# A hybrid encoder layer on one core: the last output columns in three pieces, and the scalings behind them put in another order

## The chip, the cores and the metric

The kernel runs on one core of one Trainium2 chip. The time is the device time of one execution in microseconds. Five engines work side by side, each on its own list of instructions: TensorE (PE in the profile, its weight loads PEld), VectorE (DVE), ScalarE (ACT), GpSimd (POOL) and SyncE (SP), which here only issues transfers. Engines wait for one another on semaphores.

## What is computed

One layer over 528 tokens (16 learned ones and 512 of the input) of width 2048. Cut to what matters:

```python
hn = rmsnorm(h_res, norm_in_g)              # (528, 2048)
P  = hn @ w_in                              # 2048 x 8320
y_a = rwkv7 time mixing of P[:, :4224], 16 heads of 64, gated with silu
y_b = Bg * causal_conv3(Cg * hc) * silu(g_c) of P[:, 4224:]
mix = concatenate([y_a, y_b])               # (528, 2048)
h_res = h_res + mix @ w_out                 # 2048 x 2048
out = rmsnorm(h_res, norm_f_g)[16:]         # (512, 2048), f32
```

The last line is where the change lies: each output row is scaled by one over the root of the mean of its squares (plus 1e-6), and each column by its entry of `norm_f_g`. A row's scale is known only when all its 2048 columns are.

## The kernel before

All matmuls with large operands keep f32 accuracy by splitting: an operand is `hi` (its value rounded to the type float32r) plus `lo` (the rest), and a product is three matmuls, hi by hi, hi by lo and lo by hi. The profile calls such operands f32 as well; where a cast writes one it says fp32r. One instruction on TensorE takes a weight tile of 128x128 and streams up to 512 columns over it, into a bank of PSUM.

The input projection and the recurrence take up to about 850 us, and TensorE goes through them almost without a gap. Then comes the output projection, `mix @ w_out`, in two halves of 1024 columns. Each half is a Strassen-like scheme of seven products (`M1`, `P5`, `M7`, `M3`, `Q6`, `P4`, `M2`) over blocks of 256 rows and 512 columns; a product is summed over 1024 rows of `w_out` in eight steps `jj`, three matmuls a step. `close` adds a finished product to the tiles that hold the residual: `xa[t]` for the first 1024 columns of row block `t` (four blocks of 128 tokens), `xb[m][:, t]` for the two further groups of 512. `here(t, n)` is row block `t`, column group `n` (0 to 3). `gfb` holds `norm_f_g`, the columns' factors, on all partitions.

The change is in the end of the program, from line 1400 on, behind all products but the last one, `M2` of the second half. Its weights (`right[(1, "M2", ..)]`, tiles named `home`) were split ahead of time. It adds to column group 2 of row blocks 0 and 1 only, so row blocks 2 and 3 are complete before it. The steps there:

- L1220 (called at L1403): `M2` for row block 0, 24 matmuls of 512 columns into `end`.
- `row_part` (L1364, L1365) sums the squares known so far into `fv[:, t, 0:1]`; `row_scale` (L1372, then the power at L101 on GpSimd) adds the last part and takes the power of minus one half. Its result is the row's scale `r`.
- `finish(t, ns)`: for column groups 2 and 3 one instruction on VectorE that multiplies with `r` and the factors (L1382); for group 0, which stands for the first 1024 columns, one on ScalarE (L1385), their factors having been applied earlier on GpSimd. Each is followed by its transfer to DRAM on SP's queue (L1386).
- L1411: the addition of `end` to row block 0; `squares(0, 2)` (L1207) squares it on ScalarE and sums along the row.
- L1415: the factors (`gain`, L1278) for row block 1, column group 3.
- L1416 to L1431: `M2` for row block 1 in two pieces of 256 columns, 24 matmuls each (L1422). Behind each piece its addition (L1426), its squares (L1207) and its factors (L1278). Between the two, behind the first piece, row block 0 is scaled and sent (`finish(0, (2, 0, 3))`), and L1431 adds the first piece's squares to the sum.
- `row_scale(1, 4)` on VectorE and GpSimd, and `finish_last(1)`: the four column groups of row block 1 are scaled, two on VectorE (L1391, L1396), one on ScalarE (L1393), one on GpSimd (L1395), with a transfer each, two from SP's queue (L1392, L1397) and two from ScalarE's (L1394, L1398).

The order of instructions on VectorE, ScalarE, GpSimd and TensorE is here that of the program text (`manual_schedule`); on SP it follows too. Each engine works its list strictly in order, so an instruction that waits holds up all behind it on its engine.

Of the kernel before, what the change touches and what calls it, by code (L numbers as in the profile page):

```python
# [9 lines left out]
F32 = mybir.dt.float32  # L10
# [3 lines left out]
ALU = mybir.AluOpType  # L14
# [4 lines left out]
P = 128  # L19
DM = 2048  # L20
# [56 lines left out]
def hymba_kernel(ctx: ExitStack, tc: tile.TileContext, xt, xtok, front, w_in, w_out, pv, lup, cst, msk, gf, out):  # L77
    nc = tc.nc
# [21 lines left out]
    def rsqrt(y, v):  # L100
        nc.gpsimd.tensor_tensor(out=y, in0=v, in1=mhalf[:, 0 : v.shape[1]], op=ALU.pow)  # L101
# [10 lines left out]
    for what, i in plan:  # L112
        m = tile_of[what] + i
# [109 lines left out]
    o = 0  # L223
# [61 lines left out]
    with tc.issue_after(head):  # L285
        nc.vector.tensor_scalar(
            out=omm, in0=pvt[:, V_MU : V_MU + 33], scalar1=-1.0, scalar2=1.0, op0=ALU.mult, op1=ALU.add
        )
        for d, off in (
# [4 lines left out]
                out=d, in0=pvt[:, off : off + 8], scalar1=0.5, scalar2=None, op0=ALU.mult  # L294
            )
        nc.vector.tensor_scalar(
            out=hv[:, 4], in0=pvt[:, V_KA : V_KA + 8], scalar1=-0.5, scalar2=1.0, op0=ALU.mult, op1=ALU.add
# [825 lines left out]

    pw = ctx.enter_context(tc.tile_pool(name="pw", bufs=1, reuse_waits="tile"))
    po = ctx.enter_context(tc.tile_pool(name="po", bufs=8, space=PSUM, reuse_waits="tile"))
    ssq = pw.tile([P, 4, 5], F32, name="ssq")
    fv = pw.tile([P, 4, 3], F32, name="fv")
    sform = {
        (f, q): [pw.tile([P, 4, HT], F32R, tag=f"{f}{q}{a}", name=f"{f}{q}{a}") for a in range(2)]
# [14 lines left out]
    for half in range(2):  # L1144
        units += [(half, "M1", g) for g in range(4)]
        units += [(half, prod, g) for g in range(4) for prod in ("P5", "M7", "M3", "Q6")]
        ends = ("P4", 0), ("P4", 1), ("M2", 0), ("P4", 2), ("M2", 1), ("P4", 3), ("M2", 2), ("M2", 3)
# [4 lines left out]
    def left(prod, jj, part, s):  # L1152
        w = LEFT[prod]
        tk = slice(s * P, (s + 1) * P)
        if isinstance(w, str):
            return sform[w, jj // 4][part][:, jj % 4, tk]
        if w == 0:
            return parts[jj][part][:, tk]
        return parts[NPAIR + jj][part][:, w][:, tk]
# [36 lines left out]
    def here(t, n):  # L1196
        return xa[t][:, n * 512 : (n + 1) * 512] if n < 2 else xb[n - 2][:, t]

    def onto(t, n, ps, op):
        h = here(t, n)  # L1200
        nc.vector.tensor_tensor(out=h, in0=h, in1=ps, op=op)

    def squares(t, n, part=None):
        o = slice(0, 512) if part is None else slice(256 * part, 256 * part + 256)
        sq = pw.tile([P, 512], F32, tag="sqj", name=f"sqj{n}_{t}_{part}")
        j = (0, 1, 3, 2)[n] + (part or 0)
        nc.scalar.activation(sq[:, o], here(t, n)[:, o], AF.Square, scale=DM**-0.5, accum_out=ssq[:, t, j : j + 1])  # L1207

    def gain(t, n, eng, o=slice(0, 512)):
        h = here(t, n)[:, o]  # L1210
        eng.tensor_tensor(out=h, in0=h, in1=gfb[:, n * 512 : (n + 1) * 512][:, o], op=ALU.mult)

    def product(unit, bank, s_):
        half, prod, g = unit
        for s in s_:
            for q in range(2):
                jj = 2 * g + q
                hi, lo = right[unit, q]
                for n, (m, w) in enumerate(((0, hi), (0, lo), (1, hi))):
                    nc.tensor.matmul(  # L1220
                        bank[s], left(prod, jj, m, s), w, start=(jj == 0 and n == 0), stop=(jj == 7 and n == 2)
                    )
# [4 lines left out]
    def close(half, prod, z):  # L1227
        n = 2 * half
        if prod == "M1":
            shared[:] = [pw.tile([P, 512], F32, tag=f"sh{s}", name=f"sh{half}{s}") for s in range(2)]  # L1230
        for s in range(2):
            d, p, t = shared[s], z[s], 2 + s
            if prod == "M1":
                nc.scalar.copy(d, p)
                onto(s, n, p, ALU.add)
            elif prod == "P5":
                onto(t, n + 1, p, ALU.subtract)
                onto(s, n + 1, p, ALU.subtract)
            elif prod == "M7":
                onto(t, n + 1, p, ALU.subtract)  # L1240
                onto(t, n, p, ALU.add)
            elif prod == "M3":
                onto(s, n + 1, p, ALU.subtract)
            elif prod == "Q6":
                nc.vector.tensor_tensor(out=d, in0=d, in1=p, op=ALU.add)
                for r, c, op in ((t, n, ALU.add), (t, n + 1, ALU.subtract), (s, n + 1, ALU.subtract)):
                    onto(r, c, d, op)
                squares(t, n + 1)
                squares(s, n + 1)
            elif prod == "P4":  # L1250
                onto(t, n, p, ALU.add)
                squares(t, n)
            else:
                onto(s, n, p, ALU.add)
                squares(s, n)
# [42 lines left out]
    for half in range(2):  # L1298
        o = 28 * half
# [62 lines left out]
    def row_part(t, n):  # L1362
        w = fv[:, t, 0:1]
        nc.vector.tensor_reduce(out=w, in_=ssq[:, t, 0:n], op=ALU.add, axis=AX.X)  # L1364
        nc.vector.tensor_scalar(out=w, in0=w, scalar1=RMS_EPS, scalar2=None, op0=ALU.add)  # L1365
# [3 lines left out]
    def row_scale(t, n, eng=nc.gpsimd):  # L1369
        f = fv[:, t]  # L1370
        w, v, r = f[:, 0:1], f[:, 1:2], f[:, 2:3]
        eng.tensor_scalar(out=v, in0=ssq[:, t, n : n + 1], scalar1=w, scalar2=None, op0=ALU.add)  # L1372
        rsqrt(r, v)
        scales[t] = r

    def finish(t, ns):
        r = scales[t]
        o = out[t * P : (t + 1) * P]
        for n in ns:
            if n:  # L1380
                x, a, b = here(t, n), 512 * n, 512 * n + 512
                nc.vector.scalar_tensor_tensor(out=x, in0=x, scalar=r, in1=gfb[:, a:b], op0=ALU.mult, op1=ALU.mult)  # L1382
            else:
                x, a, b = xa[t], 0, 1024
                nc.scalar.activation(x, x, AF.Copy, scale=r)  # L1385
            nc.sync.dma_start(o[:, a:b], x)  # L1386

    def finish_last(t):
        r = scales[t]
        o = out[t * P : (t + 1) * P]  # L1390
        nc.vector.tensor_scalar(out=here(t, 2), in0=here(t, 2), scalar1=r, scalar2=1.0, op0=ALU.mult, op1=ALU.mult)  # L1391
        nc.sync.dma_start(o[:, 1024:1536], here(t, 2))  # L1392
        nc.scalar.activation(here(t, 0), here(t, 0), AF.Copy, scale=r)  # L1393
        nc.scalar.dma_start(o[:, 0:512], here(t, 0))  # L1394
        nc.gpsimd.tensor_scalar(out=here(t, 3), in0=here(t, 3), scalar1=r, scalar2=1.0, op0=ALU.mult, op1=ALU.mult)  # L1395
        nc.vector.tensor_scalar(out=here(t, 1), in0=here(t, 1), scalar1=r, scalar2=1.0, op0=ALU.mult, op1=ALU.mult)  # L1396
        nc.sync.dma_start(o[:, 512:1024], here(t, 1))  # L1397
        nc.scalar.dma_start(o[:, 1536:DM], here(t, 3))  # L1398

    with tc.manual_schedule(engines={mybir.EngineType.DVE, mybir.EngineType.Activation, mybir.EngineType.Pool}):  # L1400
        end = po.tile([P, 512], F32, tag="o", name="end")
        for g in range(4):
            product((1, "M2", g), [end], (0,))  # L1403
        for t in (2, 3):
            row_part(t, 3)
            row_scale(t, 3)
        row_part(0, 3)
        row_part(1, 3)
        finish(2, (2, 0, 3))
        finish(3, (2,))  # L1410
        nc.vector.tensor_tensor(out=here(0, 2), in0=here(0, 2), in1=end, op=ALU.add)  # L1411
        squares(0, 2)
        row_scale(0, 3)
        finish(3, (0, 3))
        gain(1, 3, nc.vector)  # L1415
        ends = [po.tile([P, 256], F32, tag="o", name=f"end{part}") for part in range(2)]  # L1416
        for part in range(2):
            cols = slice(256 * part, 256 * part + 256)
            for jj in range(8):
                hi, lo = right[(1, "M2", jj // 2), jj % 2]  # L1420
                for n, (m, w) in enumerate(((0, hi), (0, lo), (1, hi))):
                    nc.tensor.matmul(  # L1422
                        ends[part], left("M2", jj, m, 1), w[:, cols], start=(jj == 0 and n == 0), stop=(jj == 7 and n == 2)
                    )
            h = here(1, 2)[:, cols]
            nc.vector.tensor_tensor(out=h, in0=h, in1=ends[part], op=ALU.add)  # L1426
            squares(1, 2, part)
            gain(1, 2, nc.vector, cols)
            if part == 0:
                finish(0, (2, 0, 3))  # L1430
                nc.vector.tensor_tensor(out=fv[:, 1, 0:1], in0=fv[:, 1, 0:1], in1=ssq[:, 1, 3:4], op=ALU.add)  # L1431
        row_scale(1, 4, nc.vector)
        finish_last(1)


# [60 lines left out]
```

## Time and profile before

| | |
|---|---|
| Time, median of 3 runs | 1019.72 us (1018.66 to 1020.17) |
| Profiled execution, its own time | 1019.89 us |
| Its span, first to last instruction | 1018.1 us |
| Mean granted TensorE clock | 0.998 |
| TensorE busy | 1005.1 us, 99% |
| VectorE, ScalarE, GpSimd busy | 684.3, 394.1, 278.2 us |
| DMA traffic | 174.82 MB, mean 172 GB/s |

The profile is of one execution. Times in it are microseconds from the start of the span unless marked ns. A row of the timeline has the start, the duration, the engine, the line of the program, the operation, the tiles written and read, their shapes and how many instructions were merged; in square brackets stands how long the engine idled before it, and who ended that. A q behind an engine's name marks its sequencer, where transfers are issued. Matmuls overlap, and the length of a single one is modelled; the spacing from start to start tells the rate.

### The profile page before, as it was taken

How to read it: one execution, taken by the hardware profiler on the slowest of the kernel's cores; microseconds unless marked ns; L12 is line 12 of the kernel's file. 1: busy time of each engine (PE TensorE's matmuls, PEld its weight loads, DVE VectorE, ACT ScalarE, POOL GpSimd, SP SyncE). 2: the span in 40 equal slices, each digit the busy share in tenths (PEclk: the TensorE clock that was granted, in tenths of full speed). 3: DMA queues.
4: the chain of work that ended last, by engine and by line, in shares of the span. 5: the costliest groups of instructions: out<-in, count | busy, mean ns of one | idle time of the engine just before them, and what ended most of it. 6: DMA issues, size and time to landing. Idle time of an engine off the chain costs nothing.

```text
span 1018.1 us, 23697 instructions
## 1 busy us (share of the span) xinstructions
PE 1005.1 (99%) x9723; PEld 918.3 (90%) x9723; DVE 684.3 (67%) x1239; ACT 394.1 (39%) x729; POOL 278.2 (27%) x292
## 2 busy tenths in 40 slices
PE   9999999999999999999999999999999999999996
PEld 8999998999998999998999998889898898787885
DVE  7777855587765669653769653244555697998787
ACT  7553423344313434323433322222222335445453
POOL 0122414233233223232323222223322332015001
PEclk9999999999999999999999999999999999999999
DMA  9426585546665263854274846777673788595754
GB/s 329 140 82 153 135 211 145 152 127 149 168 167 163 84 173 99 218 146 120 81 186 104 198 139 198 282 235 229 199 225 83 200 266 196 167 320 137 173 125 165
DMA packets 185036, 174.82 MB, mean 172 GB/s; under 512 B 121568, under 2 KB 142816, under 8 KB 184416
## 3 DMA queue, kind: packets, MB, share of 16 engines
q1 hardware_dynamic: 182336, 164.40, 56.2%
q0 software_dynamic: 2304, 8.39, 4.6%
q8 instruction: 76, 1.25, 0.5%
q10 hardware_dynamic: 288, 0.52, 0.1%
q14 instruction: 32, 0.26, 0.1%
HBM read 136.92 MB, written 36.35 MB: 170 GB/s over the span
## 4 chain that ended last, share of the span: by engine, by line
PE 84%; DVE 8%; DMA 3%; issue 2%; ACT 1%; SPq 1%; POOL 0%; DVEq 0%; ACTq 0%; POOLq 0%
PE ps_v L314 9%; PE ps_k L314 9%; PE ps_g L314 9%; PE ps_h L314 9%; PE ps_r L314 9%; PE ps_B L314 9%; PE ps_gc L314 8%; PE ps_C L314 8%; DVE ol L1193 3%; DMA wo<-in_w_out_dram 2%; PE g L659 2%; PE M L1220 2%; PE ps_lora L314 1%; PE zs L984 1%; PE Q L1220 1%
## 5 line engine op out<-in xcount | busy, mean ns | idle before, releaser
L125 POOL TENSOR_TENSOR wl<-wr,wh 128x512 fp32r<-128x512 f32 x119 | 170.9, 1438 | 369.7 <-ACT wh L124 343.8
L124 ACT CAST wh<-wr 128x512 fp32r<-128x512 f32 x252 | 152.8, 618 | 292.0 <-PE ps_C L314 49.4
L125 DVE TENSOR_TENSOR wl<-wr,wh 128x512 fp32r<-128x512 f32 x133 | 102.1, 774 | 111.8 <-ACT wh L124 102.5
L314 PE MATMUL ps_k<-xh,wh 128*128 128x264 f32 x256 | 73.2, 286 | 0.0
L314 PE MATMUL ps_v<-xh,wh 128*128 128x264 f32 x256 | 73.0, 285 | 0.0
L314 PE MATMUL ps_h<-xh,wh 128*128 128x258 f32 (+1 forms) x256 | 72.8, 284 | 0.0
L314 PE MATMUL ps_k<-xl,wh 128*128 128x264 f32 x256 | 72.7, 284 | 0.0
L314 PE MATMUL ps_v<-xh,wl 128*128 128x264 f32 x256 | 72.7, 284 | 0.0
L314 PE MATMUL ps_h<-xh,wl 128*128 128x258 f32 (+1 forms) x256 | 72.2, 282 | 0.6 <-issue 0.6
L314 PE MATMUL ps_k<-xh,wl 128*128 128x264 f32 x256 | 72.7, 284 | 0.0
L314 PE MATMUL ps_v<-xl,wh 128*128 128x264 f32 x256 | 72.6, 284 | 0.0
L314 PE MATMUL ps_C<-xh,wh 128*128 128x258 f32 (+1 forms) x256 | 72.6, 284 | 0.0
L314 PE MATMUL ps_g<-xl,wh 128*128 128x258 f32 (+1 forms) x256 | 72.3, 282 | 0.0
L314 PE MATMUL ps_r<-xl,wh 128*128 128x258 f32 (+1 forms) x256 | 72.2, 282 | 0.0
L314 PE MATMUL ps_C<-xl,wh 128*128 128x258 f32 (+1 forms) x256 | 72.1, 282 | 0.0
L314 PE MATMUL ps_g<-xh,wl 128*128 128x258 f32 (+1 forms) x256 | 72.1, 281 | 0.0
L314 PE MATMUL ps_h<-xl,wh 128*128 128x258 f32 (+1 forms) x256 | 72.0, 281 | 0.0
L314 PE MATMUL ps_g<-xh,wh 128*128 128x258 f32 (+1 forms) x256 | 72.0, 281 | 0.0
L314 PE MATMUL ps_r<-xh,wl 128*128 128x258 f32 (+1 forms) x256 | 72.0, 281 | 0.0
L314 PE MATMUL ps_r<-xh,wh 128*128 128x258 f32 (+1 forms) x256 | 72.0, 281 | 0.0
L314 PE MATMUL ps_C<-xh,wl 128*128 128x258 f32 (+1 forms) x256 | 71.9, 281 | 0.0
L314 PE MATMUL ps_gc<-xh,wl 128*128 128x512 f32 x128 | 50.9, 397 | 0.5 <-DVE wl L125 0.5
(353 smaller groups left out, 3004.8 us busy)
## 6 DMA issues: line engine op xcount, KB each, us to landing
wr<-in_w_in_dram SPq DMA_DIRECT2D x126, 512.0 KB
ct<-opd SPq DMA_DIRECT2D x64, 288.0 KB
wo<-in_w_out_dram SPq DMA_DIRECT2D x24, 512.0 KB
x<-in_w_out_dram POOLq DMA_DIRECT2D x16, 512.0 KB, 5.9
opd<-ar SPq DMA_DIRECT2D x8, 576.0 KB
opd<-gt SPq DMA_DIRECT2D x16, 288.0 KB
opd<-bt SPq DMA_DIRECT2D x64, 64.0 KB
x<-in_w_out_dram SPq DMA_DIRECT2D x8, 512.0 KB
```

Source lines behind the costliest of these rows:

```text
L124: nc.scalar.copy(hi, rq)
L125: low[q] = eng.tensor_tensor(out=lo, in0=rq, in1=hi.bitcast(F32), op=ALU.subtract).ins
L314: nc.tensor.matmul(ps[r], ww[:, w], xx[:, kt, a:b], start=(kt == 0 and n == 0), stop=(kt == KT - 1 and n == 2))
L659: nc.tensor.matmul(z[h][:, c - c0], bk[hs, c, h : h + 2, :].rearrange("p a s -> p (a s)"), ar[hs, c].rearrange("p a s -> p (a s)"), start= ...
L984: nc.tensor.matmul(d[hs, j], w, x[hs], start=(a == 0), stop=(a == b - 1))
L1193: nc.vector.tensor_tensor(out=lo, in0=rq, in1=hi.bitcast(F32), op=ALU.subtract)
L1220: nc.tensor.matmul(bank[s], left(prod, jj, m, s), w, start=(jj == 0 and n == 0), stop=(jj == 7 and n == 2))
```

## The change

Three edits, all in the last steps. First, row block 1's last 512 columns are computed in pieces of 256, 128 and 128 columns (`LAST`) instead of 256 and 256; each piece has its addition and its squares, and the squares of the first two pieces are added to the row's sum as they come. The array of sums of squares gets one more column. Second, behind the first piece only column groups 2 and 0 of row block 0 are scaled and sent; group 3 (`finish(0, (3,))`) goes behind the last piece's squares, and the columns' factors for the second and third piece are applied together, behind `row_scale`. Third, `finish_last` scales three column groups on VectorE, in the order 2, 1, 3, each with a transfer on SP's queue, and group 0 on ScalarE as before; GpSimd has none.

```diff
--- before.py
+++ after.py
@@ -1123,7 +1123,7 @@
 
     pw = ctx.enter_context(tc.tile_pool(name="pw", bufs=1, reuse_waits="tile"))
     po = ctx.enter_context(tc.tile_pool(name="po", bufs=8, space=PSUM, reuse_waits="tile"))
-    ssq = pw.tile([P, 4, 5], F32, name="ssq")
+    ssq = pw.tile([P, 4, 6], F32, name="ssq")
     fv = pw.tile([P, 4, 3], F32, name="fv")
     sform = {
         (f, q): [pw.tile([P, 4, HT], F32R, tag=f"{f}{q}{a}", name=f"{f}{q}{a}") for a in range(2)]
@@ -1200,8 +1200,11 @@
         h = here(t, n)
         nc.vector.tensor_tensor(out=h, in0=h, in1=ps, op=op)
 
+
+    LAST = (slice(0, 256), slice(256, 384), slice(384, 512))
+
     def squares(t, n, part=None):
-        o = slice(0, 512) if part is None else slice(256 * part, 256 * part + 256)
+        o = slice(0, 512) if part is None else LAST[part]
         sq = pw.tile([P, 512], F32, tag="sqj", name=f"sqj{n}_{t}_{part}")
         j = (0, 1, 3, 2)[n] + (part or 0)
         nc.scalar.activation(sq[:, o], here(t, n)[:, o], AF.Square, scale=DM**-0.5, accum_out=ssq[:, t, j : j + 1])
@@ -1388,14 +1391,12 @@
     def finish_last(t):
         r = scales[t]
         o = out[t * P : (t + 1) * P]
-        nc.vector.tensor_scalar(out=here(t, 2), in0=here(t, 2), scalar1=r, scalar2=1.0, op0=ALU.mult, op1=ALU.mult)
-        nc.sync.dma_start(o[:, 1024:1536], here(t, 2))
+        for n in (2, 1, 3):
+            x = here(t, n)
+            nc.vector.tensor_scalar(out=x, in0=x, scalar1=r, scalar2=1.0, op0=ALU.mult, op1=ALU.mult)
+            nc.sync.dma_start(o[:, 512 * n : 512 * n + 512], x)
         nc.scalar.activation(here(t, 0), here(t, 0), AF.Copy, scale=r)
         nc.scalar.dma_start(o[:, 0:512], here(t, 0))
-        nc.gpsimd.tensor_scalar(out=here(t, 3), in0=here(t, 3), scalar1=r, scalar2=1.0, op0=ALU.mult, op1=ALU.mult)
-        nc.vector.tensor_scalar(out=here(t, 1), in0=here(t, 1), scalar1=r, scalar2=1.0, op0=ALU.mult, op1=ALU.mult)
-        nc.sync.dma_start(o[:, 512:1024], here(t, 1))
-        nc.scalar.dma_start(o[:, 1536:DM], here(t, 3))
 
     with tc.manual_schedule(engines={mybir.EngineType.DVE, mybir.EngineType.Activation, mybir.EngineType.Pool}):
         end = po.tile([P, 512], F32, tag="o", name="end")
@@ -1413,23 +1414,27 @@
         row_scale(0, 3)
         finish(3, (0, 3))
         gain(1, 3, nc.vector)
-        ends = [po.tile([P, 256], F32, tag="o", name=f"end{part}") for part in range(2)]
-        for part in range(2):
-            cols = slice(256 * part, 256 * part + 256)
+        w = fv[:, 1, 0:1]
+        for part, cols in enumerate(LAST):
+            e = po.tile([P, cols.stop - cols.start], F32, tag="o", name=f"end{part}")
             for jj in range(8):
                 hi, lo = right[(1, "M2", jj // 2), jj % 2]
-                for n, (m, w) in enumerate(((0, hi), (0, lo), (1, hi))):
+                for n, (m, ww) in enumerate(((0, hi), (0, lo), (1, hi))):
                     nc.tensor.matmul(
-                        ends[part], left("M2", jj, m, 1), w[:, cols], start=(jj == 0 and n == 0), stop=(jj == 7 and n == 2)
+                        e, left("M2", jj, m, 1), ww[:, cols], start=(jj == 0 and n == 0), stop=(jj == 7 and n == 2)
                     )
             h = here(1, 2)[:, cols]
-            nc.vector.tensor_tensor(out=h, in0=h, in1=ends[part], op=ALU.add)
+            nc.vector.tensor_tensor(out=h, in0=h, in1=e, op=ALU.add)
             squares(1, 2, part)
-            gain(1, 2, nc.vector, cols)
             if part == 0:
-                finish(0, (2, 0, 3))
-                nc.vector.tensor_tensor(out=fv[:, 1, 0:1], in0=fv[:, 1, 0:1], in1=ssq[:, 1, 3:4], op=ALU.add)
-        row_scale(1, 4, nc.vector)
+                gain(1, 2, nc.vector, cols)
+                finish(0, (2, 0))
+            if part < 2:
+                nc.vector.tensor_tensor(out=w, in0=w, in1=ssq[:, 1, 3 + part : 4 + part], op=ALU.add)
+            else:
+                finish(0, (3,))
+                row_scale(1, 5, nc.vector)
+                gain(1, 2, nc.vector, slice(256, 512))
         finish_last(1)
```

## The prediction

> **What bounds the kernel now.** I read the page first. Its busy times and the chain that ended last say that TensorE is the kernel:
>
> ```profile
> PE 1005.1 (99%) x9723; PEld 918.3 (90%) x9723; DVE 684.3 (67%) x1239; ACT 394.1 (39%) x729; POOL 278.2 (27%) x292
> PE 84%; DVE 8%; DMA 3%; issue 2%; ACT 1%; SPq 1%; POOL 0%; DVEq 0%; ACTq 0%; POOLq 0%
> ```
>
> The two counts of 9723 matter below: every matmul has a weight load of its own, also where two in a row use the same weights. The change touches only the last 15 us, so the averages say nothing about it. I went to the timeline of that stretch, TensorE first (start and duration in us), and to the line of the last matmuls (shortest, median, longest in ns):
>
> ```profile
> 998.43 5.63 PE L1220 MATMUL end<-home,m 128*128 128x512 f32 x24
> 1003.90 5.91 PE L1422 MATMUL end<-home,m 128*128 128x256 f32 x48
> L1422 PEld LDWEIGHTS end<-home,m x48: 188/192/192, 1003.7 to 1009.4; 128*128 128x128 f32 x48
> L1422 PE MATMUL end<-home,m x48: 277/283/283, 1003.9 to 1009.5; 128*128 128x256 f32 x48
> ```
>
> One 512-column matmul follows another after (5.63 - 0.39) / 23 = 0.228 us (0.39 being one's length), one 256-column matmul after (5.91 - 0.28) / 47 = 0.120 us. The last ends at 1009.81. Then the other engines, in order of time:
>
> ```profile
> 1002.83 0.58 POOL L101 TENSOR_TENSOR fv<-fv,mhalf 128x1 f32<-128x1 f32 x1
> 1003.44 2.09 DVE L1382 SCALAR_TENSOR_TENSOR xb<-xb,fv,gfb 128x512 f32<-128x512 f32 x3 [0.63 <-POOL fv L101]
> 1003.78 0.85 POOL L101 TENSOR_TENSOR fv<-fv,mhalf 128x1 f32<-128x1 f32 x1
> 1005.45 0.68 DVE L1411 TENSOR_TENSOR xb<-xb,end 128x512 f32<-128x512 f32 x1
> 1006.22 0.63 ACT L1207 ACTIVATE sqj_None<-xb 128x512 f32<-128x512 f32 x1 [1.63 <-DVE xb L1411]
> ...
> 1008.29 1.14 ACT L1385 ACTIVATE xa<-xa,fv 128x1024 f32<-128x1024 f32 x1
> 1008.76 1.41 DVE L1382 SCALAR_TENSOR_TENSOR xb<-xb,fv,gfb 128x512 f32<-128x512 f32 x2
> 1009.88 1.31 SPq L1386 DMA_DIRECT2D out_dram<-xb  x2
> 1010.08 0.15 DVE L1431 TENSOR_TENSOR fv<-fv,ssq 128x1 f32<-128x1 f32 x1
> 1010.15 0.42 DVE L1426 TENSOR_TENSOR xb<-xb,end 128x256 f32<-128x256 f32 x1
> 1010.66 0.42 ACT L1207 ACTIVATE sqj<-xb 128x256 f32<-128x256 f32 x1 [1.24 <-DVE xb L1426]
> 1010.98 0.19 ACT L1207 ACTIVATION_READ_ACCUMULATOR sqj<-xb 128x1 f32 x1
> 1011.20 0.42 DVE L1278 TENSOR_TENSOR xb<-xb,gfb 128x256 f32<-128x256 f32 x1 [0.63 <-ACT sqj L1207]
> 1011.54 0.21 DVE L1372 TENSOR_SCALAR fv<-ssq,fv 128x1 f32<-128x1 f32 x1
> 1011.83 0.55 POOL L101 TENSOR_TENSOR fv<-fv,mhalf 128x1 f32<-128x1 f32 x1 [3.63 <-DVE fv L1372]
> 1012.41 0.72 ACT L1393 ACTIVATE xa<-xa,fv 128x512 f32<-128x512 f32 x1 [1.24 <-POOL fv L101]
> 1012.41 0.49 DVE L1391 TENSOR_SCALAR xb<-xb,fv 128x512 f32<-128x512 f32 x1 [0.66 <-POOL fv L101]
> 1012.48 0.98 POOL L1395 TENSOR_SCALAR xb<-xb,fv 128x512 f32<-128x512 f32 x1
> 1012.81 0.93 DVE L1396 TENSOR_SCALAR xa<-xa,fv 128x512 f32<-128x512 f32 x1
> 1012.92 0.33 SPq L1392 DMA_DIRECT2D out_dram<-xb  x1
> 1013.16 0.38 ACTq L1394 DMA_DIRECT2D out_dram<-xa  x1
> 1013.64 0.40 ACTq L1398 DMA_DIRECT2D out_dram<-xb  x1
> 1013.76 0.33 SPq L1397 DMA_DIRECT2D out_dram<-xa  x1
> ```
>
> VectorE is late by a third of a microsecond: the last result stands at 1009.81, and its addition (L1426) starts at 1010.15, behind the two scalings of row block 0. From there runs one chain: addition, squares on ScalarE, the columns' factors (L1278), the sum (L1372), the power on GpSimd (L101), and at 1012.41 the four scalings and their transfers. I call that moment T. It lies 2.60 us behind the last matmul. What follows T is transfer (duration of the stretch, busy engines, clock, DMA share, GB/s):
>
> ```profile
> 1012.40:1013.00 0.60, 0.00 (x0) 0.00 (x0) 0.59 (x2) 0.59 (x1) 0.53 (x1) 1.00 1.01 382
> 1013.00:1013.70 0.70, 0.00 (x0) 0.00 (x0) 0.70 (x1) 0.13 (x1) 0.46 (x1) 0.58 0.11 38
> 1013.70:1016.70 3.00, 0.00 (x0) 0.00 (x0) 0.04 (x1) 0.00 (x0) 0.00 (x0) 0.50 0.95 350
> ```
>
> The earlier rows drain until 1013.0, there is a hole of 0.7 us, and then the last megabyte takes 3.0 us at 350 GB/s (3.0 x 350 = 1050 KB). From T to the end of the span (1018.1) are 5.69 us.
>
> **Three pieces instead of two.** The last 256 columns become two pieces of 128, so 24 matmuls of 256 columns become 48 of 128, and with them come 24 more weight loads of full size. By columns alone one would cost 0.120 - (0.228 - 0.120) / 2 = 0.066 us and the end of TensorE would not move. No row shows a rounded-f32 matmul narrower than 256 columns. The nearest rows for a weight load that few columns hide, and for 128 columns on 128 weights, both plain f32, are:
>
> ```profile
> 45.12 0.99 PEld L438 LDWEIGHTS pss<-cs,accd 128*128 128x128 f32 x8
> 51.36 0.60 PE L454 MATMUL prs<-cs,yb 128*128 128x128 f32 x4
> 1.45 3.78 PE L173 MATMUL pwarm<-cold 128*128 128x512 f32 x4 [1.45 <-DVE cold L170]
> ```
>
> L438 streams one column per load, and its loads still come only every (0.99 - 0.19) / 7 = 0.114 us (0.19 from the loads of L1422, whose 188 to 192 ns are of the same operand size). L454's four come every (0.60 - 0.27) / 3 = 0.11 us, with 0.27 as the length of one (by L1422's 283 ns for 256 columns). I take 0.114, because that row is the load itself; the bounds for the likely case are 0.11 and the present 0.120. The 25th matmul starts at 1003.90 + 24 x 0.120 = 1006.78 as before, the 72nd now at 1006.78 + 47 x 0.114 = 1012.14, and it ends 0.23 later (0.28, less half of the 0.11 that 512 columns take longer than 256): 1012.37, that is 2.56 us later than 1009.81.
>
> The Trainium skill, page "TensorE: Matmul & The Clock Gate", section "LDWEIGHTS (loading the stationary operand)", gives a load as columns over 1.2, 107 ns for 128; the trace's 114 is near it, and by the page alone this sum would be 0.3 us smaller (an estimate).
>
> **From the last matmul to T.** The chain becomes shorter. The addition waits for TensorE, not for VectorE: it starts at about 1012.40 (0.03 for the handover, as from 1010.98 + 0.19 to 1011.20). It takes 0.28 for 128 columns (0.68 for 512, 0.42 for 256, so about 0.13 less again). The scaling of row block 0's last columns, moved here, stands next on VectorE and holds it for 0.66 (1008.76 to 1010.08 for two). Instructions there overlap by 0.07 (1010.08 + 0.15 against 1010.15), so the sum L1372 can start at 1012.40 + 0.21 + 0.66 = 1013.27. ScalarE is ready at about the same time: 0.09 to start (1010.57 to 1010.66), 0.40 for square and read-out (0.51 for 256 columns, less half of the 0.21 between 0.63 and 0.42), so 1013.17 plus 0.03. The moved scaling therefore costs 0.07 here; its cover is the square. From L1372 to T are 0.87 now. The factors for 256 columns (0.42) are put into exactly this gap, where VectorE idles 0.66 us, so they cost nothing themselves. But they run beside the power on GpSimd. The power took 0.58 beside an idle VectorE and 0.85 beside L1382, which, like the factors, reads two tiles in SBUF. I add the whole 0.28 (bounds 0 and 0.42, the whole instruction). T comes at 1013.27 + 0.87 + 0.28 = 1014.42, 2.01 later than 1012.41.
>
> The other edits here are covered. The wait of VectorE for the second piece's squares (its sum into fv) has only the last addition queued behind it, and that waits for TensorE until 1012.40: the second piece ends near 1009.7 and its squares near 1010.5. ScalarE's wide scaling (L1385) ends at 1009.43, before it is needed.
>
> **After T.** Three scalings on VectorE, spaced 0.40 (1012.41 to 1012.81), and none on GpSimd: the last ends at T + 1.29 and its transfer is issued at T + 1.31, against T + 1.35 now. L1396 took 0.93 beside GpSimd's 0.98 where L1391 took 0.49, and that goes. But the transfers set the end, one megabyte in 3.0 us, so I take 0.05 as gained (bounds 0 and 0.3). The transfer of row block 0's last columns moves from about 1010.4 to 1013.3 on SP's queue. Its 256 KB need 0.7 us; they go through between then and the first data of the last rows, about T + 1.3 = 1015.7, while nothing else is queued. Were that cover gone, it would cost the 0.7. Its issue may hold SP for 0.9 (1.31 for two), until 1014.2, before the first issue of the last rows at T + 0.5.
>
> **Sum.** 2.01 - 0.05 = 1.96 us. The profiled execution took 1019.89 us (span 1018.1, so 1.79 outside it), 0.17 above the median. It becomes 1021.85, and the median 1019.72 becomes 1021.7. The measurement can tell about 0.2% from no change, 2.04 us: this forecast lies on that edge. With 0.11 or 0.120 per matmul and the power's price between 0 and 0.42, this case spans 1021.2 to 1022.2.
>
> **Rivals.** A, the forecast: the loads bound the narrow matmuls, 64%.
>
> B: rounded f32 loses its rate below 256 columns. For it: no row shows the narrow form, and plain f32 pays passes (L173 is two matmuls in the code and four records). Against it: L454, plain f32 of 128 columns, needs only 0.11. If a 128-column matmul cost what 512 columns do, 0.228, the last would start 47 x 0.114 = 5.36 later than in A: 1027.1. 17%.
>
> C, the other side: the load does not bind and the narrow matmul costs its columns, 0.066. It decides below about 0.07. The last matmul then ends at 1006.78 + 47 x 0.066 + 0.23 = 1010.11, and the wait for the second piece's squares binds: addition at 1009.42, squares read at 1010.19, the sum, the last addition at 1010.30. T is 1010.30 + 0.21 + 0.66 + 0.87 + 0.28 = 1012.32, 0.09 earlier, and the time with the 0.05 is 1019.6, no change. Against it stand L438 and the equal counts of loads and matmuls. The same page of the Trainium skill, section "Back-to-back issue gap", has about 81 ns for a sustained 128-column stream with loads; by that the time would be about 1020.1 (an estimate), and no row here shows it. 11%.
>
> D: the load is not hidden behind so short a matmul, and both add up: 0.114 + 0.054 = 0.168, the last starts 47 x 0.054 = 2.54 later than in A: 1024.2. Against it: at 256 columns 0.114 of load and 0.108 of columns fit into 0.120. 6%.
>
> Faster by over 0.2% would need the whole chain behind TensorE to vanish without the matmuls paying: 2%.
>
> **How the numbers follow.** A, C and D together hold 81%, so the range is 1019.4 to 1024.3; B lies outside. Of A, half falls on each side of 2.04. Slower by over 0.2%: 0.33 + 0.17 + 0.06 = 0.56. Within: 0.31 + 0.11 = 0.42. Faster: 0.02.
>
> **What would show it.** 48 matmuls of 128 columns spaced 0.11 to 0.12; TensorE's last end near 1012.4; the last addition right behind it; the power at about 0.85 beside the factors; T near 1014.4; VectorE's scalings at 0.49 each; a hole in the transfers before the last megabyte, longer than 0.7 us. A spacing near 0.066 or 0.23, or an addition that starts well behind TensorE's end, would make the forecast wrong.

## The result, and the profile after

The changed kernel took 1021.12 us (median of 22 runs) against 1019.63 for the kernel before (22 runs beside it). The ratio is 1.0015, with a 95% interval of 1.0009 to 1.0021: about 1.5 us slower, from 0.9 to 2.1. That is inside the forecast's range and on its side, but under the 0.2% that the forecast took as the least that can be told from no change.

The page of the changed kernel shows 24 matmuls and 24 weight loads more, and 2.7 us more of TensorE:

```profile
span 1021.2 us, 23749 instructions
PE 1007.8 (99%) x9747; PEld 920.4 (90%) x9747; DVE 684.1 (67%) x1242; ACT 394.3 (39%) x731; POOL 277.9 (27%) x291
```

The span is 3.1 us longer than before, more than the change costs: the pieces' first matmul starts at 1005.36 here and at 1003.90 before, and nothing ahead of it was edited. In the runs below it starts anywhere from 1002.55 to 1004.20. So I compare the **tail**, from that first matmul to the end of the span: 14.22 us before, 15.85 after, 1.63 longer. The lines of the change stand a few numbers further down in this program: L1423 is the pieces' matmul, L1427 the addition, L1210 the squares, L1385 and L1281 the scaling with factors and the factors, L1433 and L1375 the sums, L1396 and L1398 the last scalings.

First TensorE, from the groups by shape (busy time, mean ns):

```profile
L1423 PE MATMUL end<-home,m 128*128 128x128 f32 x48 | 5.5, 274 | 0.0
L1423 PE MATMUL end<-home,m 128*128 128x256 f32 x24 | 3.0, 283 | 0.0
```

Then the timeline, from TensorE's pieces (the three merged under the first one's shape) and the first narrow piece's sum on:

```profile
1005.36 8.35 PE L1423 MATMUL end<-home,m 128*128 128x256 f32 x72
...
1011.88 0.16 DVE L1433 TENSOR_TENSOR fv<-fv,ssq 128x1 f32<-128x1 f32 x1 [0.53 <-ACT sqj L1210]
1013.74 0.29 DVE L1427 TENSOR_TENSOR xb<-xb,end 128x128 f32<-128x128 f32 x1 [1.70 <-PE end L1423]
1013.95 0.75 DVE L1385 SCALAR_TENSOR_TENSOR xb<-xb,fv,gfb 128x512 f32<-128x512 f32 x1
1014.12 0.31 ACT L1210 ACTIVATE sqj<-xb 128x128 f32<-128x128 f32 x1 [2.28 <-DVE xb L1427]
1014.34 0.19 ACT L1210 ACTIVATION_READ_ACCUMULATOR sqj<-xb 128x1 f32 x1
1014.61 0.21 DVE L1375 TENSOR_SCALAR fv<-ssq,fv 128x1 f32<-128x1 f32 x1
1014.73 0.42 DVE L1281 TENSOR_TENSOR xb<-xb,gfb 128x256 f32<-128x256 f32 x1
1014.90 0.66 POOL L101 TENSOR_TENSOR fv<-fv,mhalf 128x1 f32<-128x1 f32 x1 [5.12 <-DVE fv L1375]
1015.59 0.72 ACT L1398 ACTIVATE xa<-xa,fv 128x512 f32<-128x512 f32 x1 [1.06 <-POOL fv L101]
1015.59 0.49 DVE L1396 TENSOR_SCALAR xb<-xb,fv 128x512 f32<-128x512 f32 x1 [0.44 <-POOL fv L101]
```

The 48 narrow matmuls come every (5.5 - 0.27) / 47 = 0.111 us. TensorE ends 8.35 us into the tail, before at 5.91. The idle time ahead of the last addition changed its owner: VectorE was late before, and now it has done everything at 1012.04 and waits 1.70 us for TensorE. T, where the scale stands, comes 10.23 us into the tail instead of 8.51, which is 1.72 later.

Behind T, the transfers by stretch (duration, busy engines, clock, DMA share, GB/s):

```profile
1013.70:1015.60 1.90, 0.00 (x1) 0.00 (x0) 1.42 (x5) 0.42 (x3) 0.66 (x1) 1.00 0.16 59
1015.60:1016.00 0.40, 0.00 (x0) 0.00 (x0) 0.40 (x2) 0.40 (x1) 0.00 (x0) 0.95 1.03 389
1016.00:1016.90 0.90, 0.00 (x0) 0.00 (x0) 0.87 (x3) 0.31 (x1) 0.00 (x0) 0.50 0.28 102
1016.30:1016.80 0.50, 0.00 (x0) 0.00 (x0) 0.50 (x2) 0.01 (x1) 0.00 (x0) 0.50 0.01 0
1016.90:1019.80 2.90, 0.00 (x0) 0.00 (x0) 0.00 (x0) 0.00 (x0) 0.00 (x0) 0.50 0.97 362
```

Most of the first stretch is empty. The moved transfer of row block 0 goes through from about 1015.6 to 1016.3, nothing moves for 0.6 us, and the last megabyte follows from 1016.9 at 362 GB/s. From T to the end are 5.62 us, before 5.70.

### The profile page after: what moved, and what is told of

Its sections match the earlier page's. It is cut to its first block, busy times and chain, and to the rows that moved or that the text cites. A ratio compares the mean times of both kernels' runs of the same rounds, so it can differ in the third digit from the quotient of the medians.

```text
span 1021.2 us, 23749 instructions
## 1 busy us (share of the span) xinstructions
PE 1007.8 (99%) x9747; PEld 920.4 (90%) x9747; DVE 684.1 (67%) x1242; ACT 394.3 (39%) x731; POOL 277.9 (27%) x291
## 3 DMA queue, kind: packets, MB, share of 16 engines
q0 software_dynamic: 2304, 8.39, 4.8%
## 4 chain that ended last, share of the span: by engine, by line
PE 84%; DVE 8%; DMA 3%; issue 3%; ACT 1%; POOL 0%; SPq 0%; DVEq 0%; POOLq 0%; ACTq 0%
PE ps_v L314 9%; PE ps_k L314 9%; PE ps_g L314 9%; PE ps_h L314 9%; PE ps_r L314 9%; PE ps_B L314 9%; PE ps_C L314 8%; PE ps_gc L314 8%; DVE ol L1193 3%; DMA wo<-in_w_out_dram 2%; PE g L659 2%; PE M L1223 2%; PE ps_lora L314 1%; PE zs L984 1%; PE Q L1223 1%
```

## The experiments

The theory after the first look: the loads of 128 weight columns set the spacing of the narrow matmuls and make TensorE 2.4 us later, and the rest of the change gives part of that back. Its rivals: the narrow matmuls are slow for their own form, and the moves cost as much as they give.

The whole times scatter by more than these edits are worth: the 22 runs of the kernel before lie between 1018.53 and 1020.98 us. The first version below has 11 runs and the others one each, so I compare the tails of the traces, one trace for each version.

**Two pieces, the moves kept.** `LAST` has 256 and 256 columns; the last sum takes the second piece.

```diff
-    LAST = (slice(0, 256), slice(256, 384), slice(384, 512))
+    LAST = (slice(0, 256), slice(256, 512))
...
-            if part < 2:
+            if part < 1:
```

> Two pieces of 256 columns as in the kernel before, with the other two edits of the change kept (row block 0's last scaling and the factors of the second piece behind the last result, three scalings on VectorE). I measure the tail: from the first matmul of the pieces to the end of the span, 14.2 us in the kernel before, 15.8 in the changed one. Theory (the weight loads of 24 more matmuls are the whole price, the other edits shorten the chain): TensorE ends at 5.9 in the tail as before, the last addition follows at once (about 5.95, was 6.25), the scale stands at about 7.9 (was 8.5), tail 13.5 to 13.7, so about 0.6 us faster than before and 2.2 faster than changed. Rival (the moves cost as much as they give, since a scaling of 0.66 us and its transfer of 256 KB now lie behind the last result): tail 14.1 to 14.4, no change to before.

Measured: 1018.62 us against 1019.26 before, ratio 0.9994 (0.9985 to 1.0003). The times alone leave open whether it is faster than before. The tail does not: 13.64 us, 0.58 shorter than before and 2.21 shorter than in the changed kernel. Its timeline:

```profile
1004.13 5.91 PE L1423 MATMUL end<-home,m 128*128 128x256 f32 x48
...
1009.75 0.15 DVE L1433 TENSOR_TENSOR fv<-fv,ssq 128x1 f32<-128x1 f32 x1
1010.08 0.42 DVE L1427 TENSOR_TENSOR xb<-xb,end 128x256 f32<-128x256 f32 x1 [0.17 <-PE end L1423]
1010.42 0.75 DVE L1385 SCALAR_TENSOR_TENSOR xb<-xb,fv,gfb 128x512 f32<-128x512 f32 x1
...
1011.14 0.21 DVE L1375 TENSOR_SCALAR fv<-ssq,fv 128x1 f32<-128x1 f32 x1
1011.27 0.41 DVE L1281 TENSOR_TENSOR xb<-xb,gfb 128x256 f32<-128x256 f32 x1
1011.43 0.66 POOL L101 TENSOR_TENSOR fv<-fv,mhalf 128x1 f32<-128x1 f32 x1 [2.90 <-DVE fv L1375]
1012.12 0.72 ACT L1398 ACTIVATE xa<-xa,fv 128x512 f32<-128x512 f32 x1 [1.02 <-POOL fv L101]
```

TensorE ends at 5.91 as before, the addition follows at once, and T comes at 7.99 instead of 8.51. The rival falls: the moves shorten the chain. Of the versions tried, this one has the shortest tail.

**The split alone.** The kernel before, with the loop over `LAST` in three pieces; each piece keeps its factors, row block 0 is scaled behind the first piece, GpSimd keeps its scaling.

```diff
-        for part in range(2):
-            cols = slice(256 * part, 256 * part + 256)
+        for part, cols in enumerate(LAST):
...
-        row_scale(1, 4, nc.vector)
+        row_scale(1, 5, nc.vector)
```

> The kernel before with the three pieces alone; scalings, factors and last scaling stay where they were. Theory: TensorE ends at 8.35 in the tail as in the changed kernel; behind it add 0.29, squares and read-out 0.5, factors 0.22, sum to scale 0.87, so the scale at about 10.3 and a tail of 16.0, 1.8 more than before: the moves are worth only 0.1 to 0.2 us once TensorE is late. Rival (the moves carry part of the loss): tail clearly under the 15.8 of the changed kernel, 15.4 or less.

Measured: one run, 1021.99 us; tail 15.99, T at 10.28. TensorE again ends at 8.35, as its timeline shows:

```profile
1004.20 8.35 PE L1424 MATMUL end<-home,m 128*128 128x256 f32 x72
...
1012.58 0.29 DVE L1428 TENSOR_TENSOR xb<-xb,end 128x128 f32<-128x128 f32 x1 [1.30 <-PE end L1424]
```

The split alone costs 1.77 us of tail; with it, the other two edits are worth only 0.14, where without it they are worth 0.58.

**192 and 64 columns** instead of 128 and 128 in the changed kernel.

```diff
-    LAST = (slice(0, 256), slice(256, 384), slice(384, 512))
+    LAST = (slice(0, 256), slice(256, 448), slice(448, 512))
```

> The changed kernel with pieces of 256, 192 and 64 columns instead of 256, 128 and 128: the same number of matmuls, weight loads and columns. Theory (the load of 128 weight columns sets the spacing): 0.111 us from matmul to matmul in both narrow pieces, TensorE ends at 8.3 in the tail. Rival (rounded f32 under 256 columns streams at half rate, 0.111 / 128 = 0.87 ns a column): 0.167 in the piece of 192 and 0.056 in that of 64, with the same end of TensorE. The spacings tell them apart.

Measured: tail 15.76, TensorE ends at 8.32. The groups by shape:

```profile
L1423 PE MATMUL end<-home,m 128*128 128x256 f32 x24 | 3.0, 283 | 0.0
L1423 PE MATMUL end<-home,m 128*128 128x192 f32 x24 | 2.8, 274 | 0.0
L1423 PE MATMUL end<-home,m 128*128 128x64 f32 x24 | 2.8, 275 | 0.0
```

Three times as many columns in the same 2.8 us. The median spacing is 0.111 us with 192 columns and 0.112 with 64. For pieces this narrow, a price by the column streamed is ruled out.

**Half the weights.** The two narrow pieces for the first 64 tokens only; the other 64 tokens of row block 1 go without this part of the product. Each weight load then has 64 columns instead of 128, and each matmul streams as many columns as before.

```diff
+                    k = P if part == 0 else 64
-                        e, left("M2", jj, m, 1), ww[:, cols], ...
+                        e[0:k], left("M2", jj, m, 1)[:, 0:k], ww[:, cols], ...
```

> The changed kernel with the two pieces of 128 columns computed for the first 64 tokens only (the other 64 tokens of that row block don't get this product), so each weight load has 64 columns instead of 128 and each matmul streams as many columns as before. Theory (load sets the spacing, and a load of half the columns takes half): 0.06 to 0.07 us from matmul to matmul, bound by the 128 columns or the load, and TensorE ends near 6.0 in the tail instead of 8.35. Rival (half rate of narrow rounded f32 matmuls): still 0.111, TensorE ends at 8.3.

Its groups by shape (128*64 are 128 rows and 64 columns of weights):

```profile
L1424 PE MATMUL end<-home,m 128*64 128x128 f32 x48 | 3.0, 222 | 0.0
L1424 PE MATMUL end<-home,m 128*128 128x256 f32 x24 | 3.0, 283 | 0.0
```

And in its timeline all 72, the sum that waits for the second piece's squares, and the last addition:

```profile
1003.17 5.91 PE L1424 MATMUL end<-home,m 128*128 128x256 f32 x72
...
1009.38 0.16 DVE L1435 TENSOR_TENSOR fv<-fv,ssq 128x1 f32<-128x1 f32 x1 [0.53 <-ACT sqj L1210]
1009.45 0.27 DVE L1429 TENSOR_TENSOR xb<-xb,end 64x128 f32<-64x128 f32 x1
```

48 matmuls of the same 128 columns and the same type take 3.0 us instead of 5.5, 0.060 from start to start, and TensorE ends at 5.91 (tail 13.74). The narrow form is not slow: the price goes by the weight columns and not by the columns streamed. That it is the load itself, and not another step that goes by the weight columns, is the plain reading and fits L438 of the prediction, whose loads come every 0.114 us with one column streamed; no run here separates the two.

**384 and 128 columns**, in the version with two pieces.

```diff
-    LAST = (slice(0, 256), slice(256, 512))
+    LAST = (slice(0, 384), slice(384, 512))
```

> The version with two pieces and the moves, cut at column 384 instead of 256: 24 matmuls of 384 columns and 24 of 128, so half as many narrow ones as in the changed kernel and no more matmuls than in the kernel before. Theory: 0.174 and 0.111 us from matmul to matmul, TensorE ends at 24 x 0.285 + 0.2 = 7.0 in the tail (5.9 with 256 and 256), the scale at about 8.95, tail 14.6: narrow pieces cost by their unfilled loads, even without any additional matmul. Rival (the price lies in the number of matmuls, 72 against 48): TensorE ends at 5.9 and the tail is 13.5.

The groups by shape:

```profile
L1423 PE MATMUL end<-home,m 128*128 128x384 f32 x24 | 4.3, 335 | 0.0
L1423 PE MATMUL end<-home,m 128*128 128x128 f32 x24 | 2.8, 273 | 0.0
```

And in its timeline:

```profile
1003.25 6.98 PE L1423 MATMUL end<-home,m 128*128 128x384 f32 x48
...
1011.25 0.28 DVE L1281 TENSOR_TENSOR xb<-xb,gfb 128x128 f32<-128x128 f32 x1
1011.42 0.55 POOL L101 TENSOR_TENSOR fv<-fv,mhalf 128x1 f32<-128x1 f32 x1 [3.74 <-DVE fv L1375]
```

TensorE ends at 6.98, the tail is 14.51. No matmul was added to the 48 of the kernel before, and still 1.07 us are lost on TensorE: the price is the unfilled load, not the count.

T comes at 8.76, and from T to the end are 5.76 us, where the seven other traces with three last scalings on VectorE have 5.62 to 5.64. The reason is in the transfers right behind T:

```profile
1012.00:1013.40 1.40, 0.00 (x0) 0.00 (x0) 1.28 (x3) 0.72 (x1) 0.00 (x0) 1.00 1.00 370
```

Row block 0's rows, later here behind the longer first piece, keep the transfer engines fully busy until the first of the last rows come, so the moved transfer has lost its cover. I put the 0.14 us down to that; no run tries it alone.

**The third edit alone**, in the kernel before.

```diff
-        nc.gpsimd.tensor_scalar(out=here(t, 3), in0=here(t, 3), scalar1=r, ...)
+        for n in (2, 1, 3):
+            nc.vector.tensor_scalar(out=here(t, n), in0=here(t, n), scalar1=r, ...)
```

> The kernel before with the third edit alone: three scalings on VectorE and one on ScalarE at the end, none on GpSimd. Theory: the scale stands at 8.5 in the tail as before, each scaling on VectorE takes 0.48 (L1396 took 0.93 beside GpSimd), the last transfer is issued 1.4 us behind the scale as before, and the megabyte that follows takes the same time: tail 14.1 to 14.2. Rival (this edit carries most of the 0.56 us that the version with two pieces of 256 columns gained): tail 13.8 or less.

Measured: tail 13.91, between the 14.1 of the theory and the 13.8 of the rival. From T to the end are 5.62 us instead of 5.70, so the edit itself gives 0.08; the split alone, which doesn't have it, has 5.71. The other 0.22 was there before T (8.29 instead of 8.51): VectorE came to the last addition 6.02 us into the tail, not 6.25. Nothing ahead of that was edited. The timeline has the three scalings of finished rows that VectorE starts just before the pieces, the pieces, and the last addition:

```profile
1002.82 2.09 DVE L1382 SCALAR_TENSOR_TENSOR xb<-xb,fv,gfb 128x512 f32<-128x512 f32 x3 [0.63 <-POOL fv L101]
...
1003.51 5.91 PE L1420 MATMUL end<-home,m 128*128 128x256 f32 x48
...
1009.54 0.41 DVE L1424 TENSOR_TENSOR xb<-xb,end 128x256 f32<-128x256 f32 x1
```

The scalings lead the pieces by 0.69 us here and by 0.46 in the kernel before (1003.44 against 1003.90), and the last addition starts 6.72 and 6.71 us behind them. So VectorE's lateness is set by this lead, and the lead runs from 0.34 to 0.95 us over the ten traces. Two versions with a late VectorE can be compared only at the same lead.

**The factors put back** before the sum, in the version with two pieces.

```diff
+                gain(1, 2, nc.vector, slice(256, 512))
                 row_scale(1, 4, nc.vector)
-                gain(1, 2, nc.vector, slice(256, 512))
```

> The version with two pieces of 256 columns and the moves, but the second piece's factors put back before the sum and the power. Theory: the factors' 0.42 us, less the 0.07 of overlap, stand on the chain again and the power falls from 0.66 to 0.55, so the scale comes 0.23 to 0.25 later and the tail is 13.85 to 13.9. Rival (the power beside the factors loses as much as the move gives): 13.6 as without this.

The timeline behind the last squares:

```profile
1010.39 0.43 DVE L1281 TENSOR_TENSOR xb<-xb,gfb 128x256 f32<-128x256 f32 x1
1010.73 0.21 DVE L1375 TENSOR_SCALAR fv<-ssq,fv 128x1 f32<-128x1 f32 x1
1011.02 0.55 POOL L101 TENSOR_TENSOR fv<-fv,mhalf 128x1 f32<-128x1 f32 x1 [3.81 <-DVE fv L1375]
```

Measured: T at 8.22 instead of 7.99, tail 13.84 instead of 13.64. The last addition starts at 5.95 in both, so here the comparison is clean: this move is worth 0.2 us, the 0.11 that it costs the power included.

**Row block 0's last scaling put back** behind the first piece, in the same version.

```diff
-                finish(0, (2, 0))
+                finish(0, (2, 0, 3))
...
-                finish(0, (3,))
```

> The version with two pieces of 256 columns and the moves, but row block 0's last scaling and its transfer put back behind the first piece. Theory: VectorE is late again, the last addition starts at 6.25 in the tail instead of 5.95, the sum then waits for ScalarE alone, the scale comes 0.3 later and the tail is 13.9. Rival (the moved transfer of 256 KB weighs more than VectorE's lateness): tail 13.6 or less.

Measured: the last addition at 6.36 instead of 5.95, T at 8.39, tail 14.01, 0.37 more. VectorE's lateness is back:

```profile
1003.12 2.09 DVE L1385 SCALAR_TENSOR_TENSOR xb<-xb,fv,gfb 128x512 f32<-128x512 f32 x3 [0.63 <-POOL fv L101]
...
1003.46 5.91 PE L1423 MATMUL end<-home,m 128*128 128x256 f32 x48
...
1009.82 0.41 DVE L1427 TENSOR_TENSOR xb<-xb,end 128x256 f32<-128x256 f32 x1
```

The lead is 0.34 here and 0.36 in the version with two pieces (1003.77 against 1004.13), so these two can be compared. The size holds for this lead alone: the addition comes 6.70 us behind the scalings, so with a lead of about 0.75 or more it would stand at 5.95 anyway, and this move would win nothing ahead of T (an estimate). The three edits measured one by one, 0.08, 0.20 and 0.37, add up to 0.65, near the 0.58 between the kernel before and the version with two pieces, whose leads differ by 0.10.

## Why the prediction was right

The direction and the mechanism held, and the size was 0.3 us too high in the trace. All times in the table are from the first matmul of the pieces.

| step | forecast | trace |
|---|---|---|
| spacing of the narrow matmuls | 0.114 | 0.111 |
| TensorE's end | 8.47 | 8.35 |
| the last addition | 8.50 | 8.38 |
| the sum L1375 | 9.37 | 9.25 |
| from there to T | 1.15 | 0.98 |
| T | 10.52 | 10.23 |
| tail against before | +1.96 | +1.63 |

**The load.** Taken from the row of a plain-f32 load that a single column couldn't hide, 0.114, it measured 0.111, and the two runs with other widths and with half the weights show that it goes by the weight columns. The row itself has 0.112 from its second matmul on; 0.114 counts in a longer first step, 0.125 between the first two loads. Over 47 spacings, 0.1106 in the mean, the difference makes 0.16 us; the last matmul is 0.28 long where 0.23 was forecast, and TensorE's end comes 0.12 early. The rule of the Trainium skill, page "TensorE: Matmul & The Clock Gate", section "LDWEIGHTS (loading the stationary operand)", columns over 1.2, gives 107 ns for 128 columns; 111 lies between it and the row. The same page of the Trainium skill, section "Back-to-back issue gap", has 81 ns for a sustained 128-column stream. That did not appear: 111 with 128 weight columns, 60 with 64.

**The power beside the factors** was the mis-sized term. I added 0.28, from the power that ran beside a long stretch of L1382; it measured 0.66 against 0.55, so 0.11. In the row I took it from, VectorE was reading two tiles the whole time. Here the factors end 0.25 after the power's start (1014.73 + 0.42 against 1014.90). With factors of only 128 columns, which end 0.12 after it, the power took 0.55 (the run with 384 and 128): no cost at all. So the price fell with the overlap, though L1382 is also another instruction than the factors, and no run separates that from the overlap.

**The chain.** The moved scaling stood where the forecast put it and cost 0.05 against ScalarE's path (read out at 1014.53, the sum at 1014.61, less 0.03 of handover). The edit of the last scalings gave 0.08, forecast 0.05; each takes 0.48 on VectorE, where L1396 took 0.93 before.

**The transfers.** The moved 256 KB were out before the last megabyte began, so their cover held: they ran until about 1016.3, and the next data came at 1016.9. The one hole of over 0.7 us that the forecast names did not come; 0.6 us are empty behind the moved transfer, and over 1 us ahead of it. The 0.7 that a lost cover was to cost was never tried in full: in the run with 384 and 128, where row block 0's rows ran on into the last ones, T to the end was 0.14 longer.

**Rivals.** B (0.228) and D (0.168) did not happen. L454, which stood against B, was weak evidence: line 454 of the kernel is a transpose, not a product; the measured spacing excludes B by itself. C (the columns alone) came only where the load was halved: 0.060 a matmul, where C had 0.066, and there, as in its sum, the wait for the second piece's squares bound: the last addition started at 6.28, TensorE had ended at 5.91.

The chances leaned to "slower by over 0.2%" at 0.56, and that did not come. The two terms above (0.12 and 0.17), with 0.03 from the last scalings, are the difference between 1.96, on the edge, and 1.63 within it; the runs' 1.5 has both sides of the edge in its interval, barely. The measured time alone says little for the mechanism: the range from 1019.4 to 1024.3 also held C's 1019.6 and D's 1024.2. What bears the forecast out are the spacing and the steps of the table.

## What to carry to other kernels

Cutting the last piece finer shortens the steps behind it, but matmuls with 128 weight columns came here no faster than one in 0.111 us, whether they streamed 64, 128 or 192 columns. So the pieces of 128 columns made TensorE 2.4 us later, to win 0.2 between TensorE's end and T (1.88 us instead of the 2.08 with two pieces). Look first at which engine the last addition waits for: with VectorE late, the other two edits were worth 0.58 us in the traces compared, and with TensorE late 0.14. Work put beside a step that others wait for can slow that step: look in the trace at how long the two overlap. And a transfer moved to a later place needs a hole among the transfers: with 384 and 128 columns there was none.

## What was not expected of the hardware

The spacing of matmuls with 128 weight columns is the same 0.111 us at 64, 128 and 192 columns. The 0.120, 0.174 and 0.228 at 256, 384 and 512 lie on one line, which reaches 0.111 at about 235. That is an estimate of where the weight columns take over from the columns streamed: no run lies between 192 and 256, and at 128 the line's 0.066 is above the 0.060 measured with half the weights. GpSimd's power of one column took 0.28 us more beside the scalings of L1382, which kept VectorE busy all the while, 0.11 more beside an instruction of 0.42, and nothing more beside one of 0.28.
